# Start addresses of the operands of the dense products in a two-block transformer kernel: padding under and behind three pools

## The chip, the core and the metric

The kernel runs on one core of a Trainium2 chip. Its time is the device time of one execution in microseconds (us). Before the change two runs took 1493.35 and 1494.86 us, a median of 1494.11 us.

The engines are called as the profile calls them: PE is the matrix engine (TensorE), with PEld for its weight loads, DVE the vector engine, ACT the scalar engine, POOL the general engine (GpSimd) and SP the engine that issues most transfers. SBUF is the on-chip memory of 128 partitions from which the engines read; a tile begins at the same byte in every partition. PSUM holds the results of matmuls.

## The reference

The reference runs 256 tokens of width 1024, all in float32, through two blocks.

- The first block has two layers. In each, a normalised x is multiplied by `w_in` (1024 x 6856 columns); three mixers follow (stick-breaking attention, attention over the 64 best keys of an indexer, a gated recurrence), their outputs go through three branch matrices, gates and `w_out`, and are added to x. Then x = x + square(relu(h @ w_up)) @ w_down with a hidden width of 4096.
- The second block has one layer: a projection `w_in_2`, neighbourhood attention, three dilated attentions, attention to a memory of 256 rows, an output projection, and then a mixture of 32 experts (two per token) of width 512.

```
for l in range(DEPTH):
    h = rms_norm(x, norm_mix[l])
    x = x + hybrid_mixer(h, w_in[l], ...)
    h2 = rms_norm(x, norm_mlp[l])
    x = x + jnp.square(jax.nn.relu(h2 @ w_up[l])) @ w_down[l]
...
x = x + jnp.concatenate([out_na, out_dil, out_mem], axis=-1) @ w_out[l]
x = x + hierarchical_moe(rms_norm_2(x, g_ffn[l]), ...)
```

## The kernel before, in words

**Dense products.** Every product with a weight matrix outside the experts is done in split precision. A weight chunk of 1 MB lands in a tile `w` of the ring (four buffers). `split` (line 205) makes two halves of each part of it: ACT copies it into `hi` in the type float32r (line 212), DVE writes the remainder `w - hi` into `lo` (line 213). `hi` and `lo` have four buffers each in the pool `split`, of 1024 columns. The left operands have been split in the same way: the transposed x is `xh` and `xl` (8 blocks of 128 rows by 256 tokens, pool `xt`), the hidden layer is `hh` and `hl`, the mixed branches `mh` and `ml` (tiles of 4 KB, pool `p4`), the memory `memh` and `meml` (tiles of 8 KB, pool `p8`). `mm3` (line 227) then issues three matmuls for each block of 128 rows: high times high (line 230), high times low (line 231), low times high (line 232).

A matmul has a stationary operand of 128 columns, which PEld loads, and a moving operand, which PE streams. In `proj_cols` (line 280) the weights are stationary and x moves, 256 columns a time. In `proj_rows` (line 252) x is stationary and a row of the weights moves: 256, 292, 384 or 512 columns. There are 6144 such matmuls: 4464 with 256 moving columns, 1104 with 512, 384 with 384 and 192 with 292. In the profile's rows the names behind `<-` are the moving operand and the stationary one, in this order.

**Order of the work.** One instruction stream per engine, made when the kernel is built: `stream` runs the weight chunks one after the other, and between their parts `step` puts in a turn of the attention tasks, so that the dense products cover them. The loads of weights are issued by SP as ring buffers come free. The experts (32 times 6 pieces of 1 MB) are loaded into every tile that the dense part has given up, from line 1600, in `Experts`; they begin while the last dense products run.

**Memory.** Pools are laid out one behind the other: on the left the constants, small tiles, the ring, `xt`, `p4`, `p2`; on the right, from the end of SBUF downwards, `p8` and `split`. No tile is padded, so a tile begins where the one before it ends. At byte 0 lies a scratch of 2048 bytes per partition for the descriptors of transfers that POOL issues. POOL also issues the load of the router's weights, `w_r`, 1024 rows of 36 columns.

Of the kernel before, what the change touches and what calls it, by code (L numbers as in the profile page):

```python
# [10 lines left out]
F32 = mybir.dt.float32  # L11
F32R = mybir.dt.float32r
# [9 lines left out]
T = 256  # L22
# [26 lines left out]


C_MIX, C_MLP, C_MIX2, C_FFN2, C_MEM, C_LB, C_ON, C_QK, N_COLS = 0, 16, 32, 40, 48, 56, 64, 66, 72

R_QN, R_KN, R_BR, N_ROWS = 0, 128, 256, 292

# [48 lines left out]
class Core:  # L103
# [18 lines left out]
    def open_dense(self, low, high):  # L122

        pool = lambda ctx, name, bufs, **side: ctx.enter_context(
            self.tc.tile_pool(name=name, bufs=bufs, reuse_waits="tile", **side))
        self.p8 = pool(self.ctx, "p8", 3, side="right")
        self.split_p = pool(low, "split", 4, side="right")
        self.xt = pool(self.ctx, "xt", 1)
        self.p4 = pool(self.ctx, "p4", 8)
        self.p2 = pool(high, "p2", 10)  # L130
        self.new_pool = pool
# [8 lines left out]
        return self.p8.tile([128, 2048], dt, tag="s8", name=name)  # L140

    def t4(self, name, dt=F32):
        return self.p4.tile([128, 1024], dt, tag="s4", name=name)

    def t2(self, name, dt=F32):
        return self.p2.tile([128, 512], dt, tag="s2", name=name)
# [58 lines left out]
    def split(self, v):  # L205

        nc, k, n = self.nc, v.shape[1], v.shape[2]
        hi = self.split_p.tile([128, 1024], F32R, tag="hi", name="hi")
        lo = self.split_p.tile([128, 1024], F32R, tag="lo", name="lo")
        hi = hi[:, :k * n].rearrange("p (k n) -> p k n", n=n)  # L210
        lo = lo[:, :k * n].rearrange("p (k n) -> p k n", n=n)
        nc.scalar.activation(hi, v, AF.Copy)  # L212
        nc.vector.tensor_sub(lo, v, hi)  # L213
        return hi, lo
# [112 lines left out]
        return self.tiny.tile([128, n], dt, tag=f"{name}{n}", name=name)  # L327

    def x_parts(self):
        return [self.blocks(self.xt.tile([128, 8, T], F32R, tag=n, name=n)) for n in ("xh", "xl")]  # L330

    @staticmethod
    def blocks(*tiles):
# [1196 lines left out]
class Experts:  # L1530
# [10 lines left out]
    def load_router(self, low):  # L1541
        k, nc = self.k, self.nc

        self.before = k.c("sbneg")
        k.tc.keep_in_program_order(nc.gpsimd.tensor_scalar(self.before, self.before, 0.0, None, op0=ALU.is_equal))
        self.low = low
        self.pools["extra"] = k.extra
        self.w_r = self.pool(low, "router", 1).tile([128, 8, 36], F32, name="w_r")
        k.tc.keep_in_program_order(nc.gpsimd.dma_start(self.w_r, k.a["w_r"].rearrange("(k p) n -> p k n", p=128)))
        for i in range(8):  # L1550
            nc.gpsimd.tensor_scalar(self.w_r[:, i], self.w_r[:, i], k.cols[:, C_FFN2 + i:C_FFN2 + i + 1], None, op0=ALU.mult)

# [7 lines left out]
    def pool(self, ctx, name, bufs):  # L1560
        side = "right" if ctx is self.low else "left"
        return ctx.enter_context(self.k.tc.tile_pool(name=name, bufs=bufs, reuse_waits="tile", side=side))
# [5 lines left out]
    def place(self, tag, name, dt=F32):  # L1568

        n = 2 if tag == "s4" else 1  # L1570
        return [self.pools[tag].tile([128, 2048 // n], dt, tag=tag, name=name).rearrange("p (k n) -> p k n", n=512) for _ in range(n)]

    def spare(self, name, dt=F32):

# [322 lines left out]
def _biases(rpb, t5):  # L1897


    out = np.full((9, 128, 512), NEG, np.float32)  # L1900

    col = np.arange(64)
    c0 = np.clip(col - 8, 0, 48)[:, None]
    keys = np.array(WINDOWS)[col // 16][:, None] + np.arange(32)
    inside = (keys >= c0) & (keys < c0 + 16)
    at = np.clip(keys - col[:, None] + 15, 0, 30)
    near = np.where(inside[None, None], rpb[:, 4:11][:, :, at], np.float32(NEG))

    near = near.reshape(4, 2, 7, 2, 2, 16, 32)
    slabs = out[:4].reshape(4, 2, 4, 16, 2, 2, 4, 32)  # L1910
    for r in range(4):
        slabs[:, :, r] = near[:, :, 3 - r:7 - r].transpose(0, 4, 5, 1, 3, 2, 6)

    def by_distance(d, g):

        n = np.abs(d)
        nf = np.maximum(n, 1).astype(np.float32)
        large = 8 + (np.log(nf / np.float32(8)) / np.float32(math.log(1024 / 8)) * np.float32(8)).astype(np.int32)
        bucket = (d > 0) * 16 + np.where(n < 8, n, np.minimum(large, 15))
        reach = (d % DIL[g] == 0) & (n <= 64 * DIL[g])  # L1920
        return np.where(reach[..., None], t5[:, 4 * g:4 * g + 4][bucket], np.float32(NEG))

    p, key = np.arange(128)[:, None], np.arange(T)[None]
    for i in range(4):
        d = key - (p % 64 * 4 + i % 2 * 2 + p // 64)
        for h in range(2):
            out[4 + i, :, h * T:h * T + T] = by_distance(d, 0)[..., i // 2 * 2 + h]
    for g in (1, 2):
        both = by_distance(4 * (np.arange(64)[None] - p % 64), g)
        out[8].reshape(128, 8, 64)[:, 4 * g - 4:4 * g] = both.transpose(0, 2, 1)  # L1930
    return out


def _prepare(i):

    f = lambda n: np.ascontiguousarray(np.asarray(i[n]))
    by_part = lambda v: v.reshape(-1, 128).T
    a = {"x": f("x")[0]}
    a["cols"] = np.ascontiguousarray(np.concatenate(
        [by_part(f(n)) for n in ("norm_mix", "norm_mlp", "g_mix_2", "g_ffn_2", "g_mem_2", "hgrn_lb")]  # L1940
        + [np.tile(f(n).reshape(-1, 64), 2).T for n in ("hgrn_onorm", "qk_gain_2")], axis=1))
    a["rows"] = np.concatenate(
        [f(n).reshape(-1) for n in ("qn_dsa", "kn_dsa", "b_r1_2", "b_r2_2")])[None]
    a["consts"] = CONSTS
    for n in ("w_in", "w_br_sb", "w_br_dsa", "w_br_hgrn", "w_out", "w_up", "w_down"):
        a[n] = f(n)
    a["mem"] = f("mem_2")[0]
    for n in ("w_in_2", "w_mem_kv_2", "w_out_2"):
        a[n] = f(n)[0]

    pieces = np.empty((NE, 6, 128, 4, 512), np.float32)
    for j, n in enumerate(("w1_2", "w3_2")):
        pieces[:, 2 * j:2 * j + 2] = f(n)[0].reshape(NE, 2, 4, 128, 512).transpose(0, 1, 3, 2, 4)
    pieces[:, 4:] = f("w2_2")[0].reshape(NE, 4, 128, 2, 512).transpose(0, 3, 2, 1, 4)
    a["experts"] = pieces.reshape(NE, 6, 128, 2048)
    a["w_r"] = np.concatenate([f("w_r1_2")[0], f("w_r2_2")[0]], axis=1)
    a["bias"] = _biases(f("na_rpb_2")[0], f("t5_table_2"))
    return a

# [59 lines left out]
```

## Time and profile before

| what | value |
|---|---|
| median of the two runs | 1494.11 us |
| profiled execution, its own time | 1495.28 us |
| its span, first to last instruction | 1493.1 us |
| PE busy in the span | 1346.4 us (90%), 14719 matmuls |
| PEld, DVE, ACT, POOL busy | 79%, 50%, 44%, 10% |
| transfers | 376.40 MB, 252 GB/s over the span |

A row of the timeline has the start of an instruction, its length, the engine, the line and the operands. The length of a matmul there runs from its start to the end of its results, and several are under way at once; how long a matmul holds PE is seen in the distance from one start to the next. A window's row has, for each engine, its busy microseconds and its number of instructions, then PE's granted clock (1.00 is 2.4 GHz), the busy share of the transfer engines and GB/s.

### The profile page before, as it was taken

The page shows a single profiled execution, that of the slowest core. Times are in us where ns is not written, and L with a number is a line of the kernel's source. Part 1 is how long each engine was busy: PE and PEld are TensorE (multiplying, and loading weights), DVE is VectorE, ACT ScalarE, POOL GpSimd, SP SyncE. Part 2 cuts the span into 40 slices and gives each one's busy share as a digit, 9 for nine tenths or more (in the row PEclk, how much of TensorE's full clock was granted, in tenths as well). Part 3 has the DMA queues.
Part 4 walks back from the last instruction along what each step waited for, and adds up shares of the span by engine and source line. Part 5 has one row for each costly group of instructions (what it writes and reads, how often), then busy time and mean ns, then how long its engine had stood idle before and what let it go on. Part 6 is the DMA issues. An engine that isn't in the chain of part 4 may idle for free. (4 is left out here: it accounts for less than half of the span.)

```text
span 1493.1 us, 34069 instructions
## 1 busy us (share of the span) xinstructions
PE 1346.4 (90%) x14719; PEld 1182.5 (79%) x14719; DVE 746.3 (50%) x1378; ACT 661.0 (44%) x1182; POOL 153.7 (10%) x203
## 2 busy tenths in 40 slices
PE   7999999999999999999999999998777767766675
PEld 7889999989879889999898888897665655555453
DVE  6885768555565966677565565764111111111012
ACT  6664765544445556665454465863111111111111
POOL 2310011000002210020010025440000000000000
PEclk9999999999999999999999999999999978779777
DMA  9534446655546434366656657589999999999996
GB/s 298 173 108 135 133 149 201 197 182 186 197 121 198 148 95 141 109 227 209 219 180 193 234 187 182 161 330 392 387 415 417 415 417 417 416 417 415 404 418 264
DMA packets 172633, 376.40 MB, mean 252 GB/s; under 512 B 8321, under 2 KB 121137, under 8 KB 152641
## 3 DMA queue, kind: packets, MB, share of 16 engines
q1 hardware_dynamic: 169312, 366.67, 68.4%
q0 software_dynamic: 2880, 6.48, 1.5%
q8 instruction: 116, 1.90, 0.5%
q10 hardware_dynamic: 288, 1.05, 0.2%
q14 instruction: 37, 0.30, 0.1%
HBM read 372.07 MB, written 2.10 MB: 251 GB/s over the span
## 5 line engine op out<-in xcount | busy, mean ns | idle before, releaser
L213 DVE TENSOR_TENSOR lo<-w,hi 128x1024 fp32r<-128x1024 f32 (+3 forms) x334 | 387.6, 1163 | 257.5 <-ACT hi L212 256.3
L212 ACT ACTIVATE hi<-w 128x1024 fp32r<-128x1024 f32 (+3 forms) x334 | 333.4, 1001 | 318.5 <-PE ps L231 162.1
L230 PE MATMUL ps<-xh,hi 128*128 128x256 f32 x1120 | 317.4, 283 | 0.0
L232 PE MATMUL ps<-xh,lo 128*128 128x256 f32 x1120 | 312.4, 279 | 0.0
L231 PE MATMUL ps<-xl,hi 128*128 128x256 f32 x1120 | 312.3, 279 | 0.0
L1828 PE MATMUL hp<-we,xs 128*32 128x128 f32 x4096 | 154.5, 301 | 68.7 <-DMA we<-experts 57.2
L230 PEld LDWEIGHTS ps<-xh,hi 128*128 128x128 f32 x1120 | 210.4, 188 | 5.6 <-issue 3.7
L231 PEld LDWEIGHTS ps<-xl,hi 128*128 128x128 f32 x1120 | 210.4, 188 | 0.8
L232 PEld LDWEIGHTS ps<-xh,lo 128*128 128x128 f32 x1120 | 210.5, 188 | 0.0
L1828 PEld LDWEIGHTS hp<-we,xs 128*32 128x32 f32 x4096 | 122.4, 120 | 99.9 <-DMA we<-experts 67.4
L230 PE MATMUL ps<-hi,xh 128*128 128x256 f32 (+3 forms) x368 | 122.4, 334 | 0.0
L231 PE MATMUL ps<-lo,xh 128*128 128x256 f32 (+3 forms) x368 | 119.1, 325 | 0.8 <-DVE lo L213 0.8
L232 PE MATMUL ps<-hi,xl 128*128 128x256 f32 (+3 forms) x368 | 118.7, 325 | 1.2 <-DVE xl L365 1.2
L496 ACT ACTIVATE g<-hp 128x128 f32<-128x128 f32 x32 | 8.9, 277 | 224.9 <-PE hp L1828 224.9
L1869 PE MATMUL yp<-we,gT 128*32 128x128 f32 x2048 | 91.1, 335 | 18.8 <-ACT gT L1839 12.5
L230 PE MATMUL acc<-hi,hh 128*128 128x512 f32 x256 | 101.3, 396 | 0.0
L232 PE MATMUL acc<-hi,hl 128*128 128x512 f32 x256 | 101.1, 395 | 0.0
L231 PE MATMUL acc<-lo,hh 128*128 128x512 f32 x256 | 101.0, 395 | 0.0
L1869 PEld LDWEIGHTS yp<-we,gT 128*32 128x32 f32 x2048 | 71.0, 135 | 33.3 <-ACT gT L1839 20.9
L1833 DVE TENSOR_TENSOR g<-g,hp 128x128 f32<-128x128 f32 x28 | 8.1, 288 | 153.4 <-ACT g L496 153.4
L230 PEld LDWEIGHTS ps<-hi,xh 128*128 128x128 f32 x368 | 69.9, 191 | 5.3 <-issue 1.5
L232 PEld LDWEIGHTS ps<-hi,xl 128*128 128x128 f32 x368 | 69.6, 190 | 4.5 <-DVE xl L365 1.6
(530 smaller groups left out, 2024.9 us busy)
## 6 DMA issues: line engine op xcount, KB each, us to landing
we<-experts SPq DMA_DIRECT2D x155, 1024.0 KB, 17.5
w<-w_in SPq DMA_DIRECT2D x53, 1024.0 KB, 5.3
we<-experts SPq DMA_DIRECT2D x72, 512.0 KB, 15.5
w<-w_up SPq DMA_DIRECT2D x32, 1024.0 KB, 5.5
w<-w_down SPq DMA_DIRECT2D x32, 1024.0 KB, 4.9
w<-w_out SPq DMA_DIRECT2D x12, 1024.0 KB, 5.9
w<-w_in SPq DMA_DIRECT2D x36, 256.0 KB, 4.0
w<-w_in SPq DMA_DIRECT2D x8, 584.0 KB, 4.4
```

The costliest lines, as they stand in the source:

```text
L212: nc.scalar.activation(hi, v, AF.Copy)
L213: nc.vector.tensor_sub(lo, v, hi)
L230: mm(out, l[0], r[0], start=first, stop=False)
L231: mm(out, l[0], r[1], start=False, stop=False)
L232: mm(out, l[1], r[0], start=False, stop=last)
L496: ins = self.nc.scalar.activation(out, x, func, **more)
L1828: nc.tensor.matmul(hp[j * 32:j * 32 + 32, wi], xs[:, k0 + kk, es], v[kk][:, j * 128:j * 128 + 128], start=k0 + kk == 0, stop=k0 + kk == 7)
L1833: nc.vector.tensor_mul(g, g, hp[:, 1])
L1869: nc.tensor.matmul(yp[j * 32:j * 32 + 32], gT[:, kk * 32:kk * 32 + 32], v[kk][:, j * 128:j * 128 + 128], start=kk == 0, stop=kk == 3)
```

## The change

It puts unused bytes at six places. On the left, 56 floats (224 bytes) before `xt`; on the right, 120 floats (480 bytes) at the end of SBUF. The tiles of `xt` and `p4` get 8 floats (32 bytes) behind them, those of `split` 16 floats (64 bytes). The views that the instructions use keep their shape, and the experts' pieces that reuse these tiles take the same padded size. To make room, the scratch for POOL's transfers shrinks from 2048 to 1024 bytes, and `w_r` is laid out on the host as 128 rows of 288 floats, so that its load has 128 long rows in place of 1024 short ones.

In the built program the instructions of each engine stand in the same order as before, with the same waits; the load of `w_r` is the one that has another shape. What differs is where operands begin:

| operand | begins at byte, before | after | past a multiple of 64, before | after |
|---|---|---|---|---|
| `xh` | 52512 | 51712 | 32 | 0 |
| `xl` | 60704 | 59936 | 32 | 32 |
| `hi`, four buffers | 172000, then every 4096 | 171008, then every 4160 | 32 | 0 |
| `lo`, four buffers | 188384, then every 4096 | 187648, then every 4160 | 32 | 0 |
| tiles of `p4` (`hh`, `hl`, `mh`, `ml`, ...), eight | 68896, then every 4096 | 68160, then every 4128 | 32 | 0 and 32 by turns |
| tiles of `p8` (`memh`, `meml`, `mix`) | 204768, then every 8192 | 204288, then every 8192 | 32 | 0 |
| branch inputs `hg`, `ds`, `sb`, high and low | 136352 (the first) | 135872 | 32 | 0 |

Blocks within a tile lie a multiple of 512 bytes apart, so all blocks of a tile share the remainder; the exception is a chunk of 292 columns, whose rows are 1168 bytes apart (every second row is 16 bytes further). Counted over the 6144 dense matmuls, the moving operand begins 32 or 48 bytes past a multiple of 64 in all of them before; after the change it begins at a multiple of 64 in 4928 (3344 with 256 columns, 1104 with 512, 384 with 384, 96 with 292), 32 past one in 1120 (all that stream `xl`), and 16 past one in 96.

```diff
--- before.py
+++ after.py
@@ -49,6 +49,8 @@
 
 
 C_MIX, C_MLP, C_MIX2, C_FFN2, C_MEM, C_LB, C_ON, C_QK, N_COLS = 0, 16, 32, 40, 48, 56, 64, 66, 72
+
+PAD_L, PAD_R, PAD_W, PAD_X, PAD_4 = 56, 120, 16, 8, 8
 
 R_QN, R_KN, R_BR, N_ROWS = 0, 128, 256, 292
 
@@ -123,6 +125,9 @@
 
         pool = lambda ctx, name, bufs, **side: ctx.enter_context(
             self.tc.tile_pool(name=name, bufs=bufs, reuse_waits="tile", **side))
+
+        for name, n, side in (("pad_l", PAD_L, "left"), ("pad_r", PAD_R, "right")):
+            pool(self.ctx, name, 1, side=side).tile([128, n], F32, name=name)
         self.p8 = pool(self.ctx, "p8", 3, side="right")
         self.split_p = pool(low, "split", 4, side="right")
         self.xt = pool(self.ctx, "xt", 1)
@@ -140,7 +145,7 @@
         return self.p8.tile([128, 2048], dt, tag="s8", name=name)
 
     def t4(self, name, dt=F32):
-        return self.p4.tile([128, 1024], dt, tag="s4", name=name)
+        return self.p4.tile([128, 1024 + PAD_4], dt, tag="s4", name=name)[:, :1024]
 
     def t2(self, name, dt=F32):
         return self.p2.tile([128, 512], dt, tag="s2", name=name)
@@ -205,8 +210,8 @@
     def split(self, v):
 
         nc, k, n = self.nc, v.shape[1], v.shape[2]
-        hi = self.split_p.tile([128, 1024], F32R, tag="hi", name="hi")
-        lo = self.split_p.tile([128, 1024], F32R, tag="lo", name="lo")
+        hi = self.split_p.tile([128, 1024 + PAD_W], F32R, tag="hi", name="hi")
+        lo = self.split_p.tile([128, 1024 + PAD_W], F32R, tag="lo", name="lo")
         hi = hi[:, :k * n].rearrange("p (k n) -> p k n", n=n)
         lo = lo[:, :k * n].rearrange("p (k n) -> p k n", n=n)
         nc.scalar.activation(hi, v, AF.Copy)
@@ -327,7 +332,8 @@
         return self.tiny.tile([128, n], dt, tag=f"{name}{n}", name=name)
 
     def x_parts(self):
-        return [self.blocks(self.xt.tile([128, 8, T], F32R, tag=n, name=n)) for n in ("xh", "xl")]
+        return [self.blocks(self.xt.tile([128, 2048 + PAD_X], F32R, tag=n, name=n)[:, :2048].rearrange("p (k t) -> p k t", t=T))
+                for n in ("xh", "xl")]
 
     @staticmethod
     def blocks(*tiles):
@@ -1546,7 +1552,7 @@
         self.low = low
         self.pools["extra"] = k.extra
         self.w_r = self.pool(low, "router", 1).tile([128, 8, 36], F32, name="w_r")
-        k.tc.keep_in_program_order(nc.gpsimd.dma_start(self.w_r, k.a["w_r"].rearrange("(k p) n -> p k n", p=128)))
+        k.tc.keep_in_program_order(nc.gpsimd.dma_start(self.w_r.rearrange("p k n -> p (k n)"), k.a["w_r"]))
         for i in range(8):
             nc.gpsimd.tensor_scalar(self.w_r[:, i], self.w_r[:, i], k.cols[:, C_FFN2 + i:C_FFN2 + i + 1], None, op0=ALU.mult)
 
@@ -1568,7 +1574,9 @@
     def place(self, tag, name, dt=F32):
 
         n = 2 if tag == "s4" else 1
-        return [self.pools[tag].tile([128, 2048 // n], dt, tag=tag, name=name).rearrange("p (k n) -> p k n", n=512) for _ in range(n)]
+        m, pad = 2048 // n, {"s4": PAD_4, "xh": PAD_X, "xl": PAD_X}.get(tag, 0)
+        return [self.pools[tag].tile([128, m + pad], dt, tag=tag, name=name)[:, :m].rearrange("p (k n) -> p k n", n=512)
+                for _ in range(n)]
 
     def spare(self, name, dt=F32):
 
@@ -1953,7 +1961,8 @@
         pieces[:, 2 * j:2 * j + 2] = f(n)[0].reshape(NE, 2, 4, 128, 512).transpose(0, 1, 3, 2, 4)
     pieces[:, 4:] = f("w2_2")[0].reshape(NE, 4, 128, 2, 512).transpose(0, 3, 2, 1, 4)
     a["experts"] = pieces.reshape(NE, 6, 128, 2048)
-    a["w_r"] = np.concatenate([f("w_r1_2")[0], f("w_r2_2")[0]], axis=1)
+    a["w_r"] = np.ascontiguousarray(np.concatenate([f("w_r1_2")[0], f("w_r2_2")[0]], axis=1)
+                                    .reshape(8, 128, 36).transpose(1, 0, 2).reshape(128, 288))
     a["bias"] = _biases(f("na_rpb_2")[0], f("t5_table_2"))
     return a
 
@@ -2009,7 +2018,7 @@
     from concourse import bass_utils
 
     arrays = _prepare(inputs)
-    nc = bacc.Bacc("TRN2", target_bir_lowering=False, num_devices=1, dynamic_dma_scratch_size=2048)
+    nc = bacc.Bacc("TRN2", target_bir_lowering=False, num_devices=1, dynamic_dma_scratch_size=1024)
     aps = {n: nc.dram_tensor(n, v.shape, mybir.dt.from_np(v.dtype), kind="ExternalInput").ap() for n, v in arrays.items()}
     out = nc.dram_tensor("out", (T, D), F32, kind="ExternalOutput").ap()
     with tile.TileContext(nc) as tc:
```

## Rows read from the trace of the kernel before

**Rows 1.** Windows, core 0: busy us per engine, clock, transfer share, GB/s.
```profile
0.00:240.00 240.00, 230.53 (x2178) 215.79 (x2179) 172.28 (x357) 150.78 (x270) 36.50 (x53) 1.00 0.53 168
240.00:980.00 740.00, 735.85 (x5605) 672.57 (x5603) 474.00 (x744) 421.87 (x679) 101.94 (x132) 1.00 0.57 179
980.00:1040.00 60.00, 54.67 (x375) 47.93 (x373) 33.57 (x87) 31.63 (x62) 15.22 (x19) 0.96 0.97 379
1040.00:1493.00 453.00, 325.36 (x6569) 246.16 (x6567) 66.49 (x193) 56.73 (x172) 0.00 (x0) 0.84 0.98 400
```

**Rows 2.** Waits of PE, 0 to 975 us: total us, times, longest.
```profile
PE ps L360 <- DVE xn L353: 9.9, 3, 7.6
...
PE ps L231 <- DVE lo L213: 0.8, 1, 0.8
```

**Rows 3.** Groups by line and shape, PE: count, busy us, mean ns.
```profile
L230 PE MATMUL ps<-xh,hi 128*128 128x256 f32 x1120 | 317.4, 283 | 0.0
...
L230 PE MATMUL acc<-hi,hh 128*128 128x512 f32 x256 | 101.3, 396 | 0.0
...
L230 PE MATMUL ps<-hi,xh 128*128 128x384 f32 x128 | 45.3, 354 | 0.0
```

**Rows 4.** Timeline of PE, 256 columns, up-projection at 264 us: start, length.
```profile
263.74 0.28 PE L230 MATMUL ps<-xh,hi 128*128 128x256 f32 x1
...
268.84 0.28 PE L230 MATMUL ps<-xh,hi 128*128 128x256 f32 x1
```

**Rows 5.** Timeline of PE, 256 columns, up-projection at 291 us.
```profile
291.26 0.28 PE L230 MATMUL ps<-xh,hi 128*128 128x256 f32 x1
...
296.91 0.28 PE L230 MATMUL ps<-xh,hi 128*128 128x256 f32 x1
```

**Rows 6.** Timeline of PE, 512 columns: down-projection at 281, memory at 876 us.
```profile
281.11 0.40 PE L230 MATMUL acc<-hi,hh 128*128 128x512 f32 x1
...
289.51 0.40 PE L230 MATMUL acc<-hi,hh 128*128 128x512 f32 x1
...
876.53 0.39 PE L230 MATMUL ps<-hi,memh 128*128 128x512 f32 x1
...
881.97 0.39 PE L230 MATMUL ps<-hi,memh 128*128 128x512 f32 x1
```

**Rows 7.** Timeline of PE, 384 columns.
```profile
144.70 0.33 PE L230 MATMUL ps<-hi,xh 128*128 128x384 f32 x1
...
147.82 0.34 PE L230 MATMUL ps<-hi,xh 128*128 128x384 f32 x1
```

**Rows 8.** Timeline of PE, 292 columns.
```profile
33.00 0.29 PE L230 MATMUL ps<-hi,xh 128*128 128x292 f32 x1
...
36.21 0.29 PE L230 MATMUL ps<-hi,xh 128*128 128x292 f32 x1
```

**Rows 9.** Timeline of PE, 128 columns in float32r (cumulative sums of an attention).
```profile
201.27 0.22 PE L1035 MATMUL ps<-uh,sums 128*128 128x128 f32 x1
201.33 0.27 PE L1035 MATMUL ps<-ul,sums 128*128 128x128 f32 x1
```

**Rows 10.** Timeline of PE, 512 columns in plain float32 (experts' sum).
```profile
1184.41 1.45 PE L1857 MATMUL acc<-y,sgT 128*128 128x512 f32 x3
...
1185.70 1.02 PE L1857 MATMUL acc<-y,sgT 128*128 128x512 f32 x2
```

**Rows 11.** Timeline of SP's queue: issue of the experts' pieces.
```profile
970.98 8.98 SPq L1600 DMA_DIRECT2D we<-experts  x7
...
997.08 52.88 SPq L1600 DMA_DIRECT2D we<-experts  x22
```

**Rows 12.** Timeline of POOL (its issues of transfers), and `w_r`'s reader on PE.
```profile
10.17 2.68 POOL L576 DMA_DIRECT2D raw<-consts  x5
...
759.25 0.99 POOL L1549 DMA_DIRECT2D w_r<-w_r  x1
762.73 4.03 POOL L1551 TENSOR_SCALAR w_r<-w_r,cols 128x36 f32<-128x36 f32 x8 [2.49 <-DMA w_r<-w_r]
...
L1629 PE MATMUL lg_ps<-w_r,tT x32: 194/279/300, 1024.5 to 1032.5; 128*128 128x36 f32 x32
```

## The prediction

> **What bounds the kernel now.** I read the windows by stage first, then the waits of PE, then the groups by line and shape, and then the timeline for the distance between neighbouring matmuls.
>
> The windows [rows 1] show three parts. From 0 to 980 us PE is busy 966 of 980 us at a granted clock of 1.00, which is the level of 2.4 GHz, while DVE is busy 646 us (66%), ACT 573 us and the transfer engines little over half. From 1040 us on it is the other way round: transfers 0.98 at 400 GB/s, PE 325 of 453 us. Between them, from 980 to 1040 us, transfers already stand at 0.97. The first part is therefore bound by PE and the last by the experts' transfers. SP issues seven pieces at 971 us and the main stream from 997 us [rows 11], when tiles of the dense part come free, and so the end of the kernel follows the end of the dense part almost one to one.
>
> Up to 975 us PE waits for another engine about 14 us in all, most of it at the very start; for the `lo` of a weight chunk it waits once, for 0.8 us [rows 2]. So the dense stage is as long as its matmuls stand apart. The mean lengths in the groups [rows 3] (283, 396, 354 ns) say little on that, because several matmuls overlap; the distances from start to start do:
>
> - 256 columns: 45 steps in 5.10 us, 113.3 ns [rows 4]; elsewhere, with the same line, the same `xh` and the same weight buffers, 48 steps in 5.65 us, 117.7 ns [rows 5].
> - 512 columns: 36 steps in 8.40 us, 233.3 ns, and elsewhere 24 steps in 5.44 us, 226.7 ns [rows 6].
> - 384 columns: 18 steps in 3.12 us, 173.3 ns [rows 7]. 292 columns: 24 steps in 3.21 us, 133.8 ns [rows 8]. 128 columns: 60 ns [rows 9].
>
> At one column per cycle of 2.4 GHz these would be 106.7, 213.3, 160.0, 121.7 and 53.3 ns. Something costs 6 to 10% on every dense matmul, and it has two levels. Plain float32, whose 512 columns take two cycles each (426.7 ns), stands 1.29 us over three steps, 430 ns, apart [rows 10]: hardly anything is lost there, where data are read at half the rate. So the loss looks like one of reading.
>
> **What the lower level is.** Sixteen columns are 64 bytes and 6.67 ns. If PE works in stretches of 256 columns, and each line of 64 bytes that a stretch touches costs 6.67 ns, then a stretch that begins 32 bytes past a line touches 17 lines in place of 16. That gives 17 lines or 113.3 ns for 256 columns, 34 or 226.7 for 512, 17 + 9 = 26 or 173.3 for 384, 9 or 60.0 for 128, and 17 + 3 = 20 or 133.3 for 292. The rows have 113.3, 226.7, 173.3, 60 and 133.8. A loss of one cycle in sixteen columns would give 56.7 for 128 and 170.0 for 384, which the rows exclude. A fixed loss of 16 cycles per stretch begun, whatever the address, fits four rows as well and gives 135.0 for 292; the mean of 24 steps is 1.2 ns below it. One row, then, separates a loss by address from a fixed one. That is my reason to expect an effect, and its weak point.
>
> **The change part by part.**
>
> 1. *Moving operands that begin on a line.* Of the 6144 dense matmuls, 4928 lose one line per stretch: 3344 with 256 columns (6.67 ns, 22.3 us), 1104 with 512 (13.3 ns, 14.7 us), 384 with 384 (13.3 ns, 5.1 us) and 96 with 292 (6.67 ns, 0.6 us). Sum 42.7 us. The 1120 that stream `xl` stay 32 bytes off and gain nothing.
> 2. *A price that the lines may have hidden.* In plain float32 a matmul takes about 3 ns more than its columns [rows 10]; at 256 columns 17 lines explain the whole distance [rows 4], which leaves 0. I take 2.5 ns, nearer to the row in which reading is no limit: 4928 x 2.5 = 12.3 us given back, with ends of 0 and 16 us. So 30.4 us remain.
> 3. *The upper level.* It costs 4.4 ns more at 256 columns [rows 4, 5] and 6.7 ns at 512 [rows 6]. On all of them that would be 4464 x 4.4 + 1104 x 6.7 = 27 us. By the timeline about three quarters of the stage run at it (most of the MLP and the attention, not 240 to 280 or 670 to 710 us), so some 20 us. As both levels occur at the same addresses, it is no property of addresses alone; it changes only after a stall or another product, like two streams that lock in step. The new offsets between moving and stationary operands can free it or not: I take half, 10 us, with ends of 0 and 20.
> 4. *What is lost on the way.* 197 of the matmuls (101 with 384 columns, 96 with 512) come after 975 us, where transfers bound the kernel: 197 x (13.3 - 2.5) = 2 us. In the attention stages DVE is the next engine, 172 of 240 us [rows 1]; where PE now gets ahead of `lo`, the wait of 0.8 us [rows 2] grows. I take 2 us, ends 0 and 6.
> 5. *Scratch and router.* POOL issues five transfers in 2.68 us without a pause [rows 12]. With half the scratch it might have to wait for one to land; it would hold the attention's small steps behind it for a few us at 10 us into the run, when PE is still waiting for the first normalised rows. The load of `w_r` occupies POOL for 0.99 us and its first reader on POOL waits 2.49 us for it; fewer rows can shorten that, and PE reads `w_r` only at 1024 us, 258 us later [rows 12]. Both cost nothing, and even without that cover 3 us.
> 6. *Stationary operands, DVE and ACT.* The same bytes are loaded and the same elements split; the order of instructions is the same on every engine. Nothing is taken for them.
>
> Sum: 30.4 + 10 - 2 - 2 = 36 us. The profiled execution's 1495.3 us becomes 1459 us; the median of the runs is 1.2 us lower, which makes **1458 us** (-2.4%).
>
> By the Trainium skill ("TensorE: Matmul & The Clock Gate", section "Back-to-back issue gap") a matmul at full clock follows the one before it after N/2.4 + 2.5 ns; by that price the sum is the one above, and the distances of rows 4 to 9 exceed that rule throughout.
>
> **The rivals.**
>
> *Nothing changes.* The loss is fixed per stretch, and the two levels are a matter of rhythm. For it: four of five distances fit equally, and equal addresses give two levels. Against it: the 292 columns. All terms are 0: 1494 us, within 3 us. The Trainium skill speaks for this one: "SBUF — State Buffer" gives lines of 16 bytes (section "Specifications (TRN2)"), on which every operand already begins, and separate read ports for moving operand and weight load, on which PE never waits (section "Who interferes with whom"). By that rule the change could do nothing at all; but rows 4 and 5 show equal work at two speeds, which it doesn't foresee either.
>
> *Only the upper level goes.* The staggered buffers break the lock, the lower level stays as it is. 20 us, of which 2 are lost: 1476 us.
>
> *Slower: loads and streams meet more often.* Now nearly every stationary and moving operand begins exactly on a line, so a weight load and the stream beside it, which start within a few ns of each other, could ask for lines at the same moments. The price of one meeting is a line, 6.7 ns, as between the two distances of 512 columns [rows 6]. If every matmul pays it and the lines gain nothing, 6144 x 6.7 = 41 us stand in place of 20 us now: 1494 + 21 = 1515 us. It decides for "slower by 2%" only from 8 ns per matmul on, which no row shows.
>
> *The change doesn't do what it says* is excluded for the addresses, which the built program has, except for `xl`, left out above.
>
> **How the numbers follow.** Address decides the lower level, as in the sum: 0.60, around 1458, itself between 1434 (42.7 + 20 - 2 us) and 1476 (26 us, the upper level stays, 8 us lost). Nothing changes: 0.20. Only the upper level: 0.10. Slower: 0.10, up to 1515. Leaving out the best end and the worst, the range is 1438 to 1500 us. A difference of 2%, 30 us, is about what a measurement of this kernel can tell from no change. The first case lies beyond it in some seven of ten: faster by over 2% 0.43, slower by over 2% 0.04, between them 0.53. The likeliest single time is 1458.
>
> **What would show it.** Right: 256 columns with `xh` or a weight row moving 107 to 110 ns apart, 113 ns with `xl`; 512 columns 214 to 217; 384 columns 160 to 163; the experts' main stream issued at about 960 us in place of 997, and the part behind it as long as before. Wrong: distances of 113.3 or 117.7, 226.7 or 233.3, 173.3 as now. If distances shrink and the stage does not, look for new waits of PE for `lo`. A distance above 118 ns at 256 columns would mean that loads and streams collide.

## The result and the profile after

The changed kernel takes 1513.74 us (1513.38 to 1514.11) against 1494.11 us: a ratio of 1.0131, with an interval of [1.0088, 1.0175]. It is slower by some 20 us, where 36 us less had been forecast. By the bound of 2% this is no change, but the time lies outside the range of 1438 to 1500 us and on the other side. The profiled execution took 1514.1 us, its span is 1512.0 us.

The windows of the kernel after, to be held against [rows 1]; the columns are the same:

```profile
0.00:240.00 240.00, 230.28 (x2160) 215.42 (x2161) 170.23 (x353) 150.01 (x269) 36.21 (x53) 0.99 0.53 167
240.00:980.00 740.00, 723.66 (x5428) 663.89 (x5427) 457.35 (x700) 406.33 (x637) 94.07 (x124) 0.99 0.55 174
980.00:1040.00 60.00, 58.61 (x471) 51.04 (x471) 43.38 (x90) 41.76 (x87) 18.82 (x21) 1.00 0.85 300
1040.00:1512.00 472.00, 342.55 (x6665) 261.58 (x6664) 74.99 (x237) 64.10 (x191) 1.21 (x5) 0.84 0.98 402
```

By 240 us PE is 18 matmuls behind, by 980 us it is 195 behind (18 + 177), and it has been idle for 16 us of the second window in place of 4. The dense part ends later; the last dense matmul starts at 1049.2 us in place of 1028.3. The experts' part behind it is no longer than before (462.8 us from there to the end, 464.8 before). SP's queue shows the same shift: the main stream of the experts is issued 20.8 us later than in [rows 11].

```profile
991.55 8.71 SPq L1608 DMA_DIRECT2D we<-experts  x7
...
1017.84 61.66 SPq L1608 DMA_DIRECT2D we<-experts  x30
```

**Where it was lost.** I set each PE matmul of the one trace beside the same matmul of the other, since their order is the same, and followed the difference of their starts. It is 1.6 us by 30 us into the run (PE has half its clock from 14 to 17 us, a granted 0.50 where the trace of before has 1.00), creeps to 7.3 us, and then grows by 13 us in one place, between 937 and 952 us. The waits of PE up to 975 us have a first line that [rows 2] don't have:

```profile
PE ps L455 <- POOL x__10349 L1234: 11.3, 2, 8.6
...
PE ps L236 <- DVE lo L218: 0.9, 1, 0.9
```

What kept POOL shows in its own timeline. First the kernel before: four transfers `vw` (256 KB each, the rows of a window for the neighbourhood attention), then the small steps that end in the normalised `x_` (`x__10341` in the rows, `x__10349` after), on which PE works next:

```profile
911.31 2.09 POOL L1457 DMA_DIRECT2D vw<-va_rows  x3 [2.77 <-DMA va_rows<-va]
921.69 0.68 POOL L1457 DMA_DIRECT2D vw<-va_rows  x1 [8.28 <-issue]
922.44 0.91 POOL L323 TENSOR_SCALAR rs<-ms 128x8 f32<-128x8 f32 x1
...
925.19 1.05 POOL L1228 TENSOR_TENSOR x__10341<-x__10341,rs 128x512 f32<-128x512 f32 x1
```

The same stretch after:

```profile
918.72 0.73 POOL L1463 DMA_DIRECT2D vw<-va_rows  x1 [2.85 <-DMA va_rows<-va]
927.03 0.70 POOL L1463 DMA_DIRECT2D vw<-va_rows  x1 [7.58 <-issue]
933.52 0.68 POOL L1463 DMA_DIRECT2D vw<-va_rows  x1 [5.79 <-issue]
942.41 0.69 POOL L1463 DMA_DIRECT2D vw<-va_rows  x1 [8.22 <-issue]
...
945.25 1.05 POOL L1234 TENSOR_TENSOR x__10349<-x__10349,rs 128x512 f32<-128x512 f32 x1
```

Before, three `vw` go out in 2.09 us and only the fourth waits; after, each waits for the one before it to land. The trace has the landings: after, the first three land at 926.67, 933.21 and 942.11 us, and each time the next is issued 0.3 to 0.4 us later; before, the first lands at 921.34 us, and the fourth is issued at 921.69. From the first `vw` to the first `x_` it is 13.9 us before and 26.5 us after. POOL's waits in the stretch from 880 to 980 us say it in one line, before and after:

```profile
POOL vw L1457 <- issue: 8.3, 1, 8.3
```

```profile
POOL vw L1463 <- issue: 21.6, 3, 8.2
```

The first of these lines was there to be read before the change: the scratch of 2048 bytes was already full with three of these transfers under way.

Behind the idle time comes a stretch at half the clock. Windows of the kernel after around it:

```profile
935.00:940.00 5.00, 2.75 (x16) 2.42 (x14) 2.34 (x3) 1.69 (x2) 0.00 (x0) 1.00 0.89 204
940.00:946.00 6.00, 0.00 (x0) 0.00 (x0) 0.00 (x0) 0.00 (x0) 3.35 (x4) 0.69 0.67 154
946.00:952.00 6.00, 2.93 (x10) 2.64 (x11) 0.00 (x0) 0.69 (x1) 5.36 (x8) 0.50 0.07 27
```

PE issues nothing from 940 to 946 us, the granted clock falls, and 0.50 (1.2 GHz) stands for the next six. In the timeline of PE the matmuls of 384 columns then stand 0.32 us apart, in place of 0.17 as in [rows 7], until 952.5 us:

```profile
946.35 0.48 PE L455 MATMUL ps<-cst,x__10349 128*128 128x128 f32 x1 [8.60 <-POOL x__10349 L1234]
949.55 0.90 PE L455 MATMUL ps<-cst,x__10349 128*128 128x128 f32 x3 [2.72 <-POOL x__10349 L1234]
...
950.57 0.52 PE L236 MATMUL ps<-lo,xh 128*128 128x384 f32 x1
950.89 0.52 PE L237 MATMUL ps<-hi,xl 128*128 128x384 f32 x1
...
952.49 0.34 PE L236 MATMUL ps<-lo,xh 128*128 128x384 f32 x1
952.66 0.34 PE L237 MATMUL ps<-hi,xl 128*128 128x384 f32 x1
```

So 11.3 us of waiting, and 1 to 2 us of clock (seven steps 0.15 us longer, and the four small products before them), make up the 13 us.

**The distances.** Nothing of the expected 107 to 110 ns is there. Timeline of PE after, 256 columns in the up-projection, the first and the last of 23 rows of line 235 (66 steps, since each stands for three matmuls):

```profile
267.06 0.28 PE L235 MATMUL ps<-xh,hi 128*128 128x256 f32 x1
...
274.92 0.28 PE L235 MATMUL ps<-xh,hi 128*128 128x256 f32 x1
```

7.86 us over 66 steps are 119.1 ns, more than either level of [rows 4, 5]. Over the whole trace I took the mean of all starts of dense matmuls to the next start, leaving out those over 1.16 times a column per cycle (stalls and other products in between): 118.0 ns in place of 116.6 for 256 columns, 175.4 in place of 174.2 for 384, 231.8 in place of 232.7 for 512, 133.8 in place of 134.0 for 292. The shortest frequent distance at 256 is 113 in both. Of the steps at 256, 38% are 119 ns or longer after the change, 9% before.

### The profile page after: what moved, and what is told of

Same layout as the page of the kernel before. It is cut to its first block, busy times and chain, and to the rows that moved or that the text cites. A ratio compares the mean times of both kernels' runs of the same rounds, so it can differ in the third digit from the quotient of the medians.

```text
span 1512.0 us, 34069 instructions
## 1 busy us (share of the span) xinstructions
PE 1355.1 (90%) x14719; PEld 1191.9 (79%) x14719; DVE 746.0 (49%) x1378; ACT 662.2 (44%) x1182; POOL 150.3 (10%) x203
## 5 line engine op out<-in xcount | busy, mean ns | idle before, releaser
L236 PE MATMUL ps<-xl,hi 128*128 128x256 f32 x1120 | 315.7, 282 | 0.0
L237 PE MATMUL ps<-hi,xl 128*128 128x256 f32 (+3 forms) x368 | 119.6, 328 | 1.2 <-DVE xl L371 1.2
L1877 PEld LDWEIGHTS yp<-we,gT 128*32 128x32 f32 x2048 | 67.9, 131 | 32.3 <-ACT gT L1847 20.2
```

The costliest lines, as they stand in the source:

```text
L236: mm(out, l[0], r[1], start=False, stop=False)
L237: mm(out, l[1], r[0], start=False, stop=last)
L1877: nc.tensor.matmul(yp[j * 32:j * 32 + 32], gT[:, kk * 32:kk * 32 + 32], v[kk][:, j * 128:j * 128 + 128], start=kk == 0, stop=kk == 3)
```

## The experiments

Theory S (scratch): the halved scratch holds POOL at `vw`, and makes most of the loss. Theory A (addresses): the new addresses make it. Beside them stands the rule of the prediction, that each line of 64 bytes costs 6.67 ns, and its rival, a loss that is fixed. All times of this section are compared with runs of the kernel before on the same chip, a median of 1496.2 to 1496.4 us.

**e1: the scratch alone.** The kernel before, with the scratch and `w_r` of the change (its layout on the host too), no padding:

```diff
-    nc = bacc.Bacc("TRN2", target_bir_lowering=False, num_devices=1, dynamic_dma_scratch_size=2048)
+    nc = bacc.Bacc("TRN2", target_bir_lowering=False, num_devices=1, dynamic_dma_scratch_size=1024)
...
-        k.tc.keep_in_program_order(nc.gpsimd.dma_start(self.w_r, k.a["w_r"].rearrange("(k p) n -> p k n", p=128)))
+        k.tc.keep_in_program_order(nc.gpsimd.dma_start(self.w_r.rearrange("p k n -> p (k n)"), k.a["w_r"]))
```

Expected: 

> The kernel before with the scratch of 1024 bytes and the new layout of w_r, and no padding: every operand of the dense products keeps its place within 512 bytes. If the halved scratch makes most of the loss (POOL held at each vw transfer, PE then waiting for x_), the time is about 1507 us (1494 + 13), with three waits of POOL at vw and 11 us of PE's waits near 945 us. If the addresses make the loss, it is 1494 us within 3, and vw's extra waits cost nothing.

Measured: 1509.73 us, ratio 1.0098 [1.0078, 1.0117]. The dense distances are those of the kernel before (116.6, 174.1, 232.7 ns). POOL's timeline and PE's longest wait in e1:

```profile
911.88 0.74 POOL L1461 DMA_DIRECT2D vw<-va_rows  x1 [2.80 <-DMA va_rows<-va]
920.48 0.71 POOL L1461 DMA_DIRECT2D vw<-va_rows  x1 [7.85 <-issue]
927.26 0.68 POOL L1461 DMA_DIRECT2D vw<-va_rows  x1 [6.08 <-issue]
935.47 0.69 POOL L1461 DMA_DIRECT2D vw<-va_rows  x1 [7.53 <-issue]
```

```profile
PE ps L453 <- POOL x__10341 L1232: 11.2, 2, 8.4
```

That is theory S, in its size and at its place. It isn't the new load of `w_r`: the dense products of e1 are 0.5 us behind those of the kernel before at 700 us and at 900 us, with that load at 760 us between them, and 14 us behind from 935 us on.

**e2 and e5: `vw` taken off POOL.** e2 is the changed kernel, e5 is e1, both with one word changed; ACT issues the four transfers:

```diff
-                    pin(nc.gpsimd.dma_start(vw()[:, i], rows.rearrange("(r c) n -> r c n", r=4)[:, c:c + 32]))
+                    pin(nc.scalar.dma_start(vw()[:, i], rows.rearrange("(r c) n -> r c n", r=4)[:, c:c + 32]))
```

Expected of e2: 

> The changed kernel with the four vw transfers issued by ACT in place of POOL: nothing is left that could wait for scratch at 920 us. If the scratch makes 13 of the 19 us, about 1500 us (1514 - 13), and the rest is in the dense products' distances. If the addresses make all of it, 1514 us within 3. ACT waits for va_rows to land before it splits on; if that is felt, PE waits 1 to 3 us for hi near 915 us.

Expected of e5: 

> The fourth corner: no padding, as e1 (scratch 1024, new layout of w_r), with vw on ACT as in e2. If scratch and addresses add up, e1's 14 us go and the time is that of the kernel before, 1496 us within 2, with 256 columns at 116.6 ns as there; e2 then stands 3 to 4 us above it for the addresses alone. If vw on ACT gives something by itself (POOL free 8 us earlier), 1490 to 1493 us, and the staggered addresses cost 7 to 9 us.

Measured: e2 1499.48 us, 1.0025 [1.0015, 1.0034]; e5 1495.46 us, 0.9997 [0.9988, 1.0007]. The timelines of ACT and of POOL in e2:

```profile
916.15 3.09 ACTq L1463 DMA_DIRECT2D vw<-va_rows  x4
919.34 1.06 ACT L217 ACTIVATE hi<-w 128x1024 fp32r<-128x1024 f32 x1 [2.85 <-DMA vw<-va_rows]
```

```profile
924.57 0.24 POOL L328 TENSOR_SCALAR rs<-ms 128x8 f32<-128x8 f32 x1 [10.73 <-DVE ms L1232]
924.89 1.67 POOL L329 TENSOR_TENSOR rs<-rs,half 128x8 f32<-128x8 f32 x1
926.64 1.04 POOL L1234 TENSOR_TENSOR x__10349<-x__10349,rs 128x512 f32<-128x512 f32 x1
```

Four transfers go out in 3.09 us without a pause, POOL now waits for its input and not for its own queue, and the line of PE's waits for `x_` is gone. The Trainium skill agrees ("DMA: Bandwidth & Descriptors", section "SWDGE vs HWDGE vs iDMA"): descriptors of POOL's transfers are written into rings in SBUF, those of SP and ACT are not. ACT stands still for about 3 us behind the issues; PE does not feel it (0.2 us of waiting for `hi` in all).

The four corners: the padding is there or not, POOL or ACT issues `vw`, always with the scratch of 1024 bytes.

| | `vw` on POOL | `vw` on ACT | difference |
|---|---|---|---|
| no padding | 1509.7 (e1) | 1495.5 (e5) | 14.3 |
| padding of the change | 1513.7 (after) | 1499.5 (e2) | 14.3 |
| difference | 4.0 | 4.0 | |

Within the noise the two effects add: some 14 us from the scratch, through this one task, and some 4 us from the addresses. That the differences agree to a tenth is chance. The kernel after was timed beside runs of the kernel before that took 1494.1 us, the other three beside runs of 1496.2 and 1496.3; counted from those, the scratch costs 14.4 us without padding and 16.3 with it, the padding 6.1 us with POOL and 4.1 with ACT, and the interval of the kernel after alone is 13 us wide. With ACT the smaller scratch and the new `w_r` cost nothing that e5 could show.

**e3: everything on a line, nothing staggered.** Padding of 32 bytes on the left and 480 on the right only; distances between operands within 512 bytes stay those of the kernel before. From here on all kernels have e5's scratch and `vw` on ACT.

```diff
-PAD_L, PAD_R, PAD_W, PAD_X, PAD_4 = 56, 120, 16, 8, 8
+PAD_L, PAD_R, PAD_W, PAD_X, PAD_4 = 8, 120, 0, 0, 0
```

Expected: 

> Scratch 1024 and vw on ACT, and only 32 bytes before xt and 480 at the end of SBUF: all operands begin at a multiple of 64, and the distance of moving to stationary operand within 512 bytes is the same as in the kernel before, no staggering. If a line of 64 bytes costs 6.67 ns (the prediction's rule), 256 columns stand 107 to 110 ns apart and the time is about 1455 us. If the loss is fixed per stretch of 256 columns, they stand 113 or 118 ns apart as before: 1494 us within 4. If alignment to a line itself is what makes it slow in the changed kernel, 118 to 120 ns throughout: about 1502 us.

Measured: 1497.61 us, 1.0012 [1.0003, 1.0022]; 256 columns 117.2 ns, 384 174.3, 512 232.8. Its timeline where the kernel after has 119.1 ns, first and last of 23 rows (66 steps, 117.9 ns):

```profile
267.01 0.28 PE L235 MATMUL ps<-xh,hi 128*128 128x256 f32 x1
...
274.79 0.28 PE L235 MATMUL ps<-xh,hi 128*128 128x256 f32 x1
```

This refutes the rule on lines. Every moving operand, `xl` too, now begins at a multiple of 64 (save 96 with 292 columns), and not one cycle is won.

**e4: x and the weights at the same remainder.** 192 bytes on the left, nothing else, so that `xh`, `xl`, the tiles of `p4` and the split weights all begin 480 past a multiple of 512.

```diff
-PAD_L, PAD_R, PAD_W, PAD_X, PAD_4 = 56, 120, 16, 8, 8
+PAD_L, PAD_R, PAD_W, PAD_X, PAD_4 = 48, 0, 0, 0, 0
```

Expected: 

> Scratch 1024 and vw on ACT, and 192 bytes before xt only: xh, xl, the tiles of p4 and the split weights all begin at the same remainder of 512 (480), as memh and the split weights do in the kernel before, whose products always ran at the lower distance. If that relation decides between the two distances, 256 columns stand 113.3 ns apart throughout and the time falls by about 20 us to 1475. If the levels are a matter of rhythm, the mean stays near 116.6 ns: 1494 us within 4.

Measured: 1503.59 us, 1.0052 [1.0034, 1.0071]. The distance goes with this offset, but at 256 columns the wrong way: 119.7 ns, with 91% of the steps at 119 or more. At 512 columns it is the other way round, 227.7 ns in place of 232.7. Timeline of e4 for 256 columns (63 steps) and for 512 (15 steps):

```profile
267.30 0.28 PE L235 MATMUL ps<-xh,hi 128*128 128x256 f32 x1
...
274.86 0.28 PE L235 MATMUL ps<-xh,hi 128*128 128x256 f32 x1
...
287.00 0.39 PE L235 MATMUL acc<-hi,hh 128*128 128x512 f32 x1
...
290.40 0.39 PE L235 MATMUL acc<-hi,hh 128*128 128x512 f32 x1
```

120.0 and 226.7 ns: the first is 18 times 6.67 ns, the second 34 times. The move leaves every operand where it was within its 64 bytes and changes only how the stationary and the moving one lie to each other; both distances change, and in opposite directions.

**A scan of that offset.** The tiles of `p4` stay at the split weights' remainder (as in e4), `xt` and the branch inputs (`hg`, `ds`, `sb`) move, by padding at the left, behind `xt` and behind `p4`. The edit in short, with the bytes of s7 put in (`pad` lays out one unused tile of so many floats):

```diff
+        pad("pad_l", 128 // 4)
         self.p8 = pool(self.ctx, "p8", 3, side="right")
         self.split_p = pool(low, "split", 4, side="right")
         self.xt = pool(self.ctx, "xt", 1)
+        pad("pad_m", 64 // 4)
         self.p4 = pool(self.ctx, "p4", 8)
+        pad("pad_g", 256 // 4)
         self.p2 = pool(high, "p2", 10)
```

Expected of s1: 

> As e4 (scratch 1024, vw on ACT, no staggering, tiles of p4 at the split weights' remainder of 512), with xt 64 bytes ahead of the split weights in place of 0, and the branch inputs 64 behind them. 512 columns should stay at 226.7 ns as in e4. If the distance of 256 columns is set by this offset, as the staggered buffers of the changed kernel seemed to show for odd multiples of 64 (113.5 ns, against 118.6 to 120 for even ones), x moving stands at 113 to 114 ns and the time is about 1503.6 - 4464 x 6 ns = 1477 us. If only offset 0 is special, 117 ns and about 1491 us; if the offset decides nothing, 119.7 ns and 1504 us.

Expected of s2: 

> As s1, with xt 128 bytes ahead of the split weights and the branch inputs at 0. If even multiples of 64 are bad, x moving stands at 118.6 to 120 ns and the time is 1499 to 1504 us; if only offset 0 is, 117 ns and about 1491 us, and the branch inputs then stand at 119.8 ns as x does in e4.

Expected of s4: 

> As s1, with xt 256 bytes ahead of the split weights and the branch inputs 64. If even multiples of 64 are bad, 118.6 to 120 ns and 1499 to 1504 us; if the offset acts as a time until stream and load meet, half a period of 512 bytes away should be the best or the worst: 113.3 ns and 1475 us, or 120 ns and 1504 us.

Expected of s7: 

> As s1, with xt 64 bytes behind the split weights (448 ahead of them within 512) and the branch inputs 128 ahead. If odd multiples of 64 are good, 113 to 114 ns and about 1477 us. If the sign of the offset matters (the load runs after the stream or ahead of it), s1 and s7 differ, one at 113 ns, the other at 118 to 120 (1477 against 1500 us).

After these four, three more:

Expected of s3: 

> As s1, with xt 192 bytes ahead of the split weights and the branch inputs 128 behind. By the parity of 64 bytes seen so far (odd 115.7 to 117.5 ns, even 119.1 to 119.8) x moving stands at 115.5 to 117.5 ns and the time is 1488 to 1495 us; the branch inputs, even, stand near 118.7. If parity is a coincidence of the offsets tried, 119 ns and 1502 us.

Expected of u_xm32: 

> As s1, with xt 32 bytes behind the split weights and the branch inputs 32 ahead: a distance of half a line. If every odd multiple of 32 breaks the meeting of loads and streams, 113.3 ns throughout and about 1470 us (1488 - 4464 x 2.5 ns and some). If half a line touches both lines, it is as slow as the even offsets, 119 to 120 ns and 1502 us; in the changed kernel xl, 32 bytes off, stood at 119.3 ns, which speaks for this.

Expected of u_xp32: 

> As u_xm32, with xt 32 bytes ahead of the split weights (and so at a multiple of 512). Same two outcomes: 113.3 ns and 1470 us, or 119 to 120 ns and 1502 us. If the sign matters as between s1 (117.5 ns) and s7 (115.8), this one is the slower of the two by 1 to 2 ns, 5 to 8 us.

Measured; "x" is where `xt` begins, counted from the split weights, within 512 bytes. The means (ns) are worked out as above; "sum" is the difference to e5 that these means give over 4464, 384 and 1104 matmuls (us), and beside it stands the measured one.

| run | x | 256 col., `xh` moving | 256 col., all | 384 | 512 | time, us | ratio, interval | sum | measured |
|---|---|---|---|---|---|---|---|---|---|
| e5 | 320 | 116.7 | 116.5 | 174.2 | 232.7 | 1495.5 | 0.9997 [0.9988, 1.0007] | | |
| e2 | staggered | 117.7 | 118.0 | 175.4 | 231.8 | 1499.5 | 1.0025 [1.0015, 1.0034] | +5.9 | +4.0 |
| e3 | 320 | 117.6 | 117.2 | 174.3 | 232.8 | 1497.6 | 1.0012 [1.0003, 1.0022] | +3.0 | +2.1 |
| e4 | 0 | 119.8 | 119.7 | 174.2 | 227.7 | 1503.6 | 1.0052 [1.0034, 1.0071] | +8.5 | +8.1 |
| s2 | 128 | 119.1 | 119.2 | 175.8 | 228.7 | 1502.2 | 1.0045 [1.0030, 1.0059] | +8.2 | +6.7 |
| s4 | 256 | 119.8 | 119.6 | 174.1 | 227.6 | 1502.2 | 1.0044 [1.0028, 1.0060] | +8.1 | +6.8 |
| s1 | 64 | 117.5 | 117.6 | 174.4 | 228.6 | 1495.0 | 0.9989 [0.9978, 1.0001] | 0.0 | -0.4 |
| s3 | 192 | 115.9 | 116.5 | 173.5 | 227.5 | 1489.0 | 0.9948 [0.9930, 0.9967] | -6.2 | -6.5 |
| s7 | 448 | 115.8 | 116.3 | 173.5 | 227.5 | 1487.7 | 0.9937 [0.9915, 0.9960] | -7.2 | -7.7 |
| u_xm32 | 480 | 118.3 | 118.1 | 174.9 | 228.7 | 1497.2 | 1.0010 [1.0000, 1.0019] | +2.9 | +1.8 |
| u_xp32 | 32 | 116.9 | 117.5 | 173.8 | 228.6 | 1493.9 | 0.9983 [0.9974, 0.9993] | -0.4 | -1.5 |

At even multiples of 64 (0, 128, 256) `xh` moving stands 119.1 to 119.8 ns apart, at odd ones (64, 192, 320, 448) 115.8 to 117.6, in every run. The branch inputs repeat the difference, though it is smaller in places: 120.0 ns at 0 (`ds` and `sb` of s2), 118.7 at 128 and 384 (s7, e4), 117.3 to 118.1 at 64, 192 and 448 (s4, e5, s1). The tiles of `p4` are a control: the weights that stream past `mh` and `ml`, 256 columns a time, lie at 320 in e5 and at 0 in e4 and all seven kernels of the scan. They stand 114.9 ns apart in e5 and 119.7 to 119.9 in the other eight, wherever x lies; past `hh` and `hl`, at the same two offsets, 512 columns stand 233.3 ns apart in e5 and 226.9 to 227.6 in the other eight. So the mean distance of a product goes with the offset of its own two operands, and something that acts on the whole kernel alike doesn't explain it. s3, for which the order by parity had been foreseen, came out as foreseen. What was expected of the odd offsets, 113.3 ns throughout, came at none of them: also there two levels alternate, and only their shares differ. In s7 42% of the steps are at 115 ns or less, in e5 28%, in e4 2%. The two half lines came out at neither of the expected values, and u_xp32, expected the slower of the two if the sign matters, is the faster by 1.4 ns and 3 us. A theory of the meeting that gives these numbers I don't have.

Timeline of s7 at the place where e4 has 120.0 and 226.7 ns: 63 steps and 42 steps, 113.3 and 226.7.

```profile
267.08 0.28 PE L242 MATMUL ps<-xh,hi 128*128 128x256 f32 x1
...
274.22 0.28 PE L242 MATMUL ps<-xh,hi 128*128 128x256 f32 x1
...
279.68 0.39 PE L242 MATMUL acc<-hi,hh 128*128 128x512 f32 x1
...
289.20 0.39 PE L242 MATMUL acc<-hi,hh 128*128 128x512 f32 x1
```

In s7 the experts' main stream (the second of these rows) is issued at 989.86 us, 7.2 us before that of the kernel before [rows 11]:

```profile
963.84 8.69 SPq L1615 DMA_DIRECT2D we<-experts  x7
...
989.86 47.74 SPq L1615 DMA_DIRECT2D we<-experts  x19
```

s7 beats both kernels: 0.6% faster than the one before, some 26 us faster than the change; s3, at 1489.0 us, can't be told apart from it. Of its 7.7 us over e5 about 5.7 come from 512 columns (1104 times 5.2 ns). It is a version with uniform offsets, with POOL out of the way, and none of its dense operands begins on a line of 64 bytes.

## Why the prediction was wrong

- **Step 1, moving operands that begin on a line: failed.** It was worth 42.7 us and gave nothing; e3 shows it with every operand aligned. The arithmetic of 17 lines for 256 columns fitted rows that a fixed 16 cycles per stretch fitted as well. One row, 292 columns [rows 8], was to tell the two apart by 1.2 ns. That mean is 134.0 ns in the kernel before and in e3 alike, and between 132.3 (s2) and 134.4 ns (u_xp32) in all these kernels, so it could not carry the choice. A chance of 0.60 was too much for it.
- **Step 2, the hidden price, and step 4, what is lost on the way:** with no gain in step 1 there was nothing for them to take from.
- **Step 3, the upper level: right that offsets between the operands act on it, wrong in its sign.** In place of 10 us given back, the staggered buffers made 38% of the steps at 256 columns 119 ns or longer. 4464 times 1.45 ns (e2 against e5) are 6.5 us lost, 1.0 us came back at 512 columns, and 4.0 us are what the time shows. I had taken it that new offsets could only break a lock; they also make one, and a stagger meets good and bad offsets by turns. The step's ground, that both levels occur at the same addresses, holds for 256 columns [rows 4, 5] and not for 512: [rows 6] set `hh` at an offset of 320 beside `memh` at 0, and e4, with `hh` at 0, has 227.4 ns for it in place of 233.3.
- **Step 5, scratch and router, "Both cost nothing": failed, and it is the larger part, 14.3 us.** The step named the right mechanism, that POOL might have to wait for a transfer to land, and looked at the wrong transfers. `raw` [rows 12] lost only this much after the change, at a time when nobody waited (e5 has the same wait, 1.82 us, and its dense products are 0.1 us behind those of the kernel before at 30 us):

```profile
9.59 2.16 POOL L582 DMA_DIRECT2D raw<-consts  x4
13.63 0.55 POOL L582 DMA_DIRECT2D raw<-consts  x1 [1.89 <-issue]
```

  The transfers that counted are the four `vw` at 911 us, at a place where POOL's steps behind them feed PE. I went by the waits of PE and passed over a row among those of POOL, which I had read too: 8.3 us at "issue", which said that the scratch was full before it was halved. The other half of the step held: the load of `w_r` cost nothing (e1, e5).
- **Step 6, stationary operands: their loads take as long as before (189 ns in the mean, 188 before), but where they begin matters,** since the distance goes with the offset between them and the stream.
- **The rivals.** "Nothing changes" was nearest in that alignment does nothing (e3); its fixed loss does not hold, since 256 columns stand 113.3 to 120.0 ns apart with the offset. The rule that it drew on, separate read ports on which PE never waits (the Trainium skill, "SBUF — State Buffer", section "Who interferes with whom"), does not agree with e4 and s7: the same products stand 120.0 and 113.3 ns apart there, and only padding differs. The measurement decides. "Loads and streams meet more often" had the right sign and its sign of recognition, a distance above 118 ns, but the size of 21 us was five times too large (4.0 us, e2 against e5), and exactly equal beginnings are not special: 128 and 256 bytes are as bad. That its 1515 us lies beside the measured 1513.7 is luck, since some 14 of the 20 us are the scratch's, for which it had no term. "Only the upper level goes" did not come: the longer distances became more frequent.
- **The check at the end** named the distances that would show step 1 wrong, 113.3 or 117.7, 226.7 or 233.3, 173.3, and the stage shows those and longer ones.

What stays open: why the parity of 64 bytes acts at 256 columns, why 512 columns go by another order (with x stationary 228.0 to 229.2 ns at 0, 192, 256 and 448, 232.6 to 233.3 at 32, 64, 128, 320 and 480), and what decides between the levels at one and the same offset. For the scratch, what a transfer takes of it wasn't measured: with 1024 bytes seven transfers are under way at once at 11.7 us in the kernel after (four of them `raw`), of `vw` only one.

## What to carry to other kernels

Before a resource for an engine's transfers is made smaller, read that engine's own waits at "issue" over the whole run, not one sample of its transfers: here every such wait at a transfer, `vw` or `raw`, ended 0.3 to 0.4 us after an earlier transfer of POOL had landed, so a single such row said that the scratch was full, and then the question is what stands behind it on that queue and who waits for that. Room for padding can be dearer than the padding is worth; here moving four issues to another engine took the price away. Offsets between stationary and moving operands are worth a scan with uniform shifts (up to 16 us between the best and the worst here, 1.1%), but not a rule worked out from distances that two rules fit.

## What the runs showed of the hardware

- In split precision at full clock 256 columns stood 113.3, 117 to 118 or 120.0 ns apart in steady stretches, and how often each came went with the offset between the stationary operand's and the moving operand's start; 512 columns stood 226.7 to 233 ns apart. Shifting both together by 32 bytes (e3 against e5) moved the mean by 0.7 ns only.
- No offset tried brought 256 columns below 113 ns in a steady stretch; a column per cycle would be 106.7.
- `vw` transfers of 256 KB: with the scratch of 2048 bytes three were under way at once from POOL, with 1024 one, and the issue of the next then held POOL for 5.8 to 8.2 us, until 0.3 to 0.4 us after the landing. From ACT four went out in 3.09 us.
